# Rearranging the GpSimd work, two weight sums, the product order and the start of a ReGLU MLP kernel

## The chip, the cores and the metric

The kernel runs on one core of one Trainium2 chip. The metric is the device time of one execution in microseconds (us). Every kernel here was also run once under the hardware profiler; the page, timeline and waits quoted below are from that execution, and their times count from its first instruction.

Engines: PE is TensorE's matmuls (PEld its weight loads), DVE is VectorE, ACT is ScalarE, POOL is GpSimd, SP is the engine that issues most transfers. In the profile's lines, SPq is SP's sequencer.

## The reference

```python
batch, seq, dim, hidden = 16, 256, 512, 2048      # x 4096x512, w1 512x4096, w2 2048x512, float32

def reference(x, w1, w2):
    h = x @ w1
    gate, value = np.split(h, 2, axis=-1)
    h = np.maximum(gate, 0) * value
    return (h @ w2).astype(np.float32)
```

## The kernel before

The kernel computes in float16 with Strassen's scheme: seven products P1 to P7 in place of eight, for sums of blocks of the weights (T1 to T4) and of x or g (S1 to S4). The 4096 rows are taken in four rounds of 1024. A round has a first matmul (16 blocks of 7 products, x times w1, giving g) and a second matmul, called mm2 (4 pairs of 7 products, g times w2). While TensorE works, the other engines form the sums, evict the PSUM tiles, check that the values fit float16's range, and fetch the next round's x.

The next round's x comes in two transfers: GpSimd starts a "cast" (float32 in HBM to a float16 copy in HBM, 1024 rows each), and then SP starts eight transposing loads from that copy. The range checks on x (`look`) read the same float16 copies.

```python
    def look(t, at):                       # range check of 256 rows of x, all on GpSimd
        n, m = t.shape[1:]
        fold = tmp.tile([P, n, m], F32, name="fold", tag="fold", bufs=1)
        nc.gpsimd.tensor_tensor(fold, t, t, op=MULT)
        while m > 2:
            m //= 2
            nc.gpsimd.tensor_tensor(fold[:, :, :m], fold[:, :, :m], fold[:, :, m:2 * m], op=ADD)
        nc.gpsimd.tensor_tensor(st[:, at:at + n], fold[:, :, 0], fold[:, :, 1], op=ADD)

    def sums_of(o, eng=nc.vector):         # S sums: VectorE, or GpSimd where eng says so
        for n, i0, i1, op in (("S1", "A21", "A22", ADD), ("S2", "S1", "A11", SUB), ("S4", "A12", "S2", SUB),
                              ("S3", "A11", "A21", SUB)):
            yield eng.tensor_tensor(o[n], o[i0], o[i1], op=op)
    # [...]
    def look_x(s, i):
        look(load_rows(s, i), 32 * s + 8 * i)      # the rows are fetched where the check stands
    # [...]
    for n, at in enumerate([(1, jb) for jb in (0, 2, 4, 6, 13)] + [(2, jb) for jb in (0, 2, 4, 6, 13)] +
                           [(3, jb) for jb in range(6)]):
        LOOKX[at] = n // 4, n % 4
    CASTS = {(0, 12): 1, (1, 0): 0, (1, 1): 2, (1, 8): 3}      # (round, block): which 1024 rows are cast
    SUMS = (9, 10, 11, 12)                                     # blocks of the next round's x sums on GpSimd
    SUMS_AT = (10, 11, 13, 15), (22, 26, 36, 40), (46, 53, 57, 61), (70, 78, 82, 87)   # steps of the S sums in mm2
    # [...] in the loop over the first matmul of round 0:
                    if 6 <= todo < 10:                         # w2's four blocks, loaded by GpSimd
                        n2 = ("B11", "T3", "B22", "B21")[todo - 6]
                        nc.gpsimd.dma_start(out=vop[n2], in_=w2_v[(0, 0, 1, 1)[todo - 6], (0, 1, 1, 0)[todo - 6]])
                    if todo == len(wl):
                        nc.gpsimd.tensor_tensor(vop["T1"], vop["T3"], vop["B11"], op=SUB)
                        nc.gpsimd.tensor_tensor(vop["T2"], vop["B22"], vop["T1"], op=SUB)
                        for j in range(0, NPLAIN, 2):
                            plain_w_end(j, 2)                  # four sums of 128x512 on GpSimd
                        nc.gpsimd.tensor_tensor(vop["T3"], vop["B22"], vop["T3"], op=SUB)
    # [...]
    ORDER = ("P1 0, P1 1, P2 0, P2 1, P1 2, P5 0, P2 2, P6 0, P3 0, P7 0, P5 1, P6 1, P4 0, P3 1, P7 1, P5 2, P4 1, "
             "P6 2, P3 2, P7 2, P1 3, P4 2, P5 3, P2 3, P6 3, P3 3, P7 3, P4 3")   # mm2: product, pair
```

The start of round 0 is special: x is transposed on TensorE (`turn_first`), and the first two blocks use eight ordinary products per half of the rows (`Plain`) because no sums are ready yet.

```python
    turn_first(xo, 0, 0, new_w())
    turn_first(xo, 0, 1, new_x())
    rest()
    ys = [psy.tile([P, TH], F32, name="Y", tag="Y") for _ in range(3)]
    plain[0].products(0, *first_half, half)
    turn_first(xo, 0, 2, new_x())
    turn_first(xo, 0, 3, ys[0])
    plain[0].products(0, *first_half, other)
    # [...] second half likewise; clear(ys[i]) are three filler matmuls
```

## Time and profile before

| | before |
|---|---|
| median of 4 runs | 325.98 us (324.76 to 326.54) |
| profiled span | 323.4 us |
| TensorE busy | 305.7 us, 95% |
| first product of the Strassen kind | 18.88 us |
| first mm2 begins | 63.12 us |
| mm2 stretch of rounds 1, 2, 3 | 28.46, 29.86, 24.45 us |
| first-matmul stretch of rounds 2, 3 | 48.65, 48.64 us |

An "mm2 stretch" runs from the first product of mm2 to the first product of the next round; a "first-matmul stretch" from there to the next mm2. They are read from the starts of TensorE's rows in the timeline. Rounds 1 to 3 do the same TensorE work in mm2, so round 3, which has no idle time, shows the length that the others could have.

The first mm2 in the timeline of the kernel before. Columns: start, duration, engine, line, operation, output and inputs, count; in brackets the idle time before it and what ended it.

```profile
66.53 0.61 PE L314 MATMUL X<-v_B_95,g 128*128 128x256 f16 x4 [1.07 <-DMA v_B_95<-in_w_dram]
...
67.70 4.05 POOL L555 TENSOR_TENSOR v_T_99<-v_B_96,v_T_99 128x2048 f16<-128x2048 f16 x1
...
68.39 3.91 DVE L160 TENSOR_TENSOR w_stage<-g 128x1024 f16<-128x1024 f16 x1
...
72.36 1.05 PE L314 MATMUL W<-v_T_97,w_stage 128*128 128x256 f16 x8 [2.61 <-DVE w_stage L160]
72.39 0.69 DVE L160 TENSOR_TENSOR w_stage<-w_stage,g 128x1024 f16<-128x1024 f16 x1
```

Compare the two VectorE rows: the same operation on the same shapes takes 3.91 us while GpSimd's T3 sum runs, and 0.69 us right after it. The VectorE sum ends within 0.6 us of GpSimd's. TensorE waits 2.61 us for it.

The second mm2 in the timeline of the kernel before:

```profile
147.02 2.57 POOL L160 TENSOR_TENSOR x_S_1145<-x_A_1140,x_S_1145 128x1024 f16<-128x1024 f16 x1
147.64 2.50 DVE L160 TENSOR_TENSOR w_stage<-g,w_stage 128x1024 f16<-128x1024 f16 x1
...
150.19 1.05 PE L314 MATMUL W<-v_B_96,w_stage 128*128 128x256 f16 x8 [1.48 <-ACT sq L175]
151.96 5.87 POOL L169 TENSOR_TENSOR fold<-fold 128x512 f32<-128x512 f32 x6
152.49 1.47 PE L314 MATMUL Y<-v_T_99,w_stage 128*128 128x256 f16 x8 [1.25 <-DVE w_stage L160]
...
154.16 1.89 PE L314 MATMUL W<-v_T_97,w_stage 128*128 128x256 f16 x8 [0.20 <-DVE w_stage L160]
```

GpSimd is still busy with x sums and one late check, VectorE's sums last 2.5 us, TensorE idles, and after the idling a group of eight matmuls lasts 1.89 us instead of 1.05: its clock has dropped. The wait at 150.19 is put down to ScalarE, but these matmuls do not read what that ScalarE row (a range check on w1) wrote; they read `w_stage`, and the VectorE sum that ends at 150.14 is the one to look at.

### The profile page before, as it was taken

To read this page: it belongs to the slowest core of one execution; us is meant where nothing else is said; L and a number is where in the kernel's file an instruction comes from. 1 tells how busy PE (TensorE), PEld (TensorE's weight loads), DVE (VectorE), ACT (ScalarE), POOL (GpSimd) and SP (SyncE) were. 2 spreads that over 40 slices of the span, in tenths; PEclk is the share of its full clock that TensorE was granted. 3 is DMA by queue.
4 is the path that set the end of the run, shared out by engine and by line. 5 is a ranking of instruction groups with operands and counts; after the bars stand their busy time and mean duration, and the time that the engine had idled before them with its cause. 6 is when DMAs were issued, how large, how long until landed. Compare 5 with 4: busy or idle time off the path is not lost.

```text
span 323.4 us, 5208 instructions
## 1 busy us (share of the span) xinstructions
PE 305.7 (95%) x1870; PEld 183.5 (57%) x1870; DVE 239.0 (74%) x372; ACT 175.7 (54%) x350; POOL 166.1 (51%) x191
## 2 busy tenths in 40 slices
PE   7879999959999999996999999999999999999992
PEld 3744444548864444464785444448885444447882
DVE  1478888879748888889935888888735888898741
ACT  2468886516675555534476455554676555553230
POOL 2299999990024008999505179991005898700000
PEclk9999999999999999999899999999999999999998
DMA  8985758978536252060224430000235300000223
GB/s 247 356 252 184 238 90 110 197 105 170 183 117 130 53 134 77 2 130 0 90 107 132 100 127 3 0 1 2 84 113 172 89 2 1 0 2 1 84 80 105
DMA packets 37199, 32.90 MB, mean 102 GB/s; under 512 B 14384, under 2 KB 32048, under 8 KB 37040
## 3 DMA queue, kind: packets, MB, share of 16 engines
q1 hardware_dynamic: 31760, 25.70, 25.8%
q0 software_dynamic: 4352, 6.29, 11.6%
q10 hardware_dynamic: 1056, 0.52, 0.6%
q8 instruction: 16, 0.26, 0.4%
q14 instruction: 15, 0.12, 0.1%
HBM read 27.26 MB, written 12.58 MB: 123 GB/s over the span
## 4 chain that ended last, share of the span: by engine, by line
PE 73%; POOL 9%; DMA 8%; DVE 5%; issue 3%; SPq 0%; ACT 0%; DVEq 0%; POOLq 0%
PE Y L229 20%; PE W L229 13%; PE X L229 13%; PE Y L314 12%; PE W L314 8%; PE X L314 7%; DVE w_stage L160 4%; DMA v_B_95<-in_w_dram 4%; POOL w_T_90 L211 3%; POOL w_T_91 L212 3%; POOL w_T_93 L214 2%; DMA w_stage<-in_w_dram 2%; DMA x_S_122<-in_x_dram 2%; POOL w_T_92 L213 0%; DVE g L266 0%
## 5 line engine op out<-in xcount | busy, mean ns | idle before, releaser
L166 POOL TENSOR_TENSOR fold<-xh 128x1024 f32<-128x1024 f16 x16 | 30.7, 1920 | 93.6 <-DMA xh<-x_1069 43.3
L256 DVE SCALAR_TENSOR_TENSOR cc<-W,pu 128x512 f32<-128x512 f32 x62 | 42.9, 691 | 32.3 <-ACT pu L250 29.8
L314 PEld LDWEIGHTS <-w_stage 128*128 128x128 f16 x512 | 50.4, 99 | 13.7 <-DVE w_stage L160 7.4
L169 POOL TENSOR_TENSOR fold<-fold 128x512 f32<-128x512 f32 (+2 forms) x96 | 54.0, 562 | 7.5
L236 ACT COPY Y<-X 128x512 f32<-128x512 f32 x62 | 35.4, 570 | 38.4 <-PE X L229 22.3
L250 ACT ACTIVATE pu<-Y 128x512 f32<-128x512 f32 x62 | 37.0, 597 | 35.2 <-PE Y L229 34.1
L266 DVE SCALAR_TENSOR_TENSOR g<-Y,cc 128x512 f16<-128x512 f32 x62 | 42.2, 681 | 4.3 <-PE Y L229 4.3
L257 DVE SCALAR_TENSOR_TENSOR g<-X,cc 128x512 f16<-128x512 f32 x62 | 42.9, 691 | 2.3
L314 PEld LDWEIGHTS <-g 128*128 128x128 f16 x384 | 37.5, 98 | 9.5 <-DMA v_B_95<-in_w_dram 1.3
L262 DVE SCALAR_TENSOR_TENSOR cc<-Y,pu 128x512 f32<-128x512 f32 x62 | 42.2, 681 | 0.1
L243 ACT ACTIVATE pu<-W 128x512 f32<-128x512 f32 x62 | 37.4, 603 | 0.4 <-DVE g L257 0.4
L160 DVE TENSOR_TENSOR w_stage<-g 128x1024 f16<-128x1024 f16 x32 | 27.2, 878 | 0.2
L229 PEld LDWEIGHTS <-w_B_89 128*128 128x128 f16 x124 | 12.0, 98 | 15.8 <-DVE x_S_153 L160 1.6
L229 PEld LDWEIGHTS <-w_T_93 128*128 128x128 f16 x124 | 12.0, 97 | 15.3 <-issue 2.5
L229 PEld LDWEIGHTS <-w_T_91 128*128 128x128 f16 x124 | 12.1, 98 | 15.0 <-issue 0.5
L229 PEld LDWEIGHTS <-w_T_90 128*128 128x128 f16 x124 | 12.1, 98 | 14.7
L229 PEld LDWEIGHTS <-w_B_88 128*128 128x128 f16 x124 | 12.1, 98 | 14.5 <-issue 0.6
L229 PEld LDWEIGHTS <-w_T_92 128*128 128x128 f16 x124 | 12.1, 98 | 14.2 <-POOL w_T_91 L212 0.6
L314 PE MATMUL W<-v_T_97,w_stage 128*128 128x256 f16 x128 | 17.5, 282 | 2.8 <-DVE w_stage L160 2.8
L229 PEld LDWEIGHTS <-w_B_87 128*128 128x128 f16 x124 | 12.0, 96 | 13.3
L314 PE MATMUL Y<-v_T_99,w_stage 128*128 128x256 f16 x128 | 17.0, 277 | 1.3 <-DVE w_stage L160 1.3
L314 PE MATMUL W<-v_B_96,w_stage 128*128 128x256 f16 x128 | 16.6, 273 | 1.5 <-ACT sq L175 1.5
(220 smaller groups left out, 578.3 us busy)
## 6 DMA issues: line engine op xcount, KB each, us to landing
out_dram<-o SPq DMA_DIRECT2D x31, 256.0 KB, 2.0
w_stage<-in_w_dram SPq DMA_DIRECT2D x14, 512.0 KB, 5.3
x_625<-in_x_dram POOLq DMA_DIRECT2D x1, 1024.0 KB, 10.4
x_1069<-in_x_dram POOLq DMA_DIRECT2D x1, 1024.0 KB, 7.9
xh<-x_1069 SPq DMA_DIRECT2D x4, 256.0 KB, 3.4
x_1112<-in_x_dram POOLq DMA_DIRECT2D x1, 1024.0 KB, 7.4
xh<-x_625 SPq DMA_DIRECT2D x4, 256.0 KB, 3.0
x_1344<-in_x_dram POOLq DMA_DIRECT2D x1, 1024.0 KB, 7.5
```

Source lines behind the costliest of these rows:

```text
L160: yield eng.tensor_tensor(o[n], o[i0], o[i1], op=op)
L166: nc.gpsimd.tensor_tensor(fold, t, t, op=MULT)
L169: nc.gpsimd.tensor_tensor(fold[:, :, :m], fold[:, :, :m], fold[:, :, m:2 * m], op=ADD)
L229: nc.tensor.matmul(ps, wop[wn][:, b, self.jb * P:(self.jb + 1) * P], self.xo[xn][:, b, :], start=fresh and b == 0, stop=b == 1, skip_group ...
L236: nc.scalar.copy(out=self.Y, in_=self.X)
L243: nc.scalar.activation(self.p5, self.W, COPY, scale=GS)
L250: nc.scalar.activation(self.u2, self.Y, COPY, scale=GS)
L256: nc.vector.scalar_tensor_tensor(out=self.c12, in0=self.W, scalar=GS, in1=self.u2, op0=MULT, op1=ADD)
L257: nc.vector.scalar_tensor_tensor(out=self.g[:, self.jb, :TH], in0=self.X, scalar=0.0, in1=self.c12, op0=MAX, op1=MULT)
L262: nc.vector.scalar_tensor_tensor(out=self.c22, in0=self.Y, scalar=GS, in1=self.p5, op0=MULT, op1=ADD)
L266: nc.vector.scalar_tensor_tensor(out=self.g[:, self.jb, TH:], in0=self.Y, scalar=0.0, in1=self.c22, op0=MAX, op1=MULT)
L314: nc.tensor.matmul(ps, self.op[an][:, i], vop[wn][:, i], start=name in ("P1", "P5") and i == 0, stop=i == NJ // 2 - 1, skip_group_check=True)
```

## The change

Its intent is to leave GpSimd idle during mm2. Checks follow one another early in the first matmul, with their rows fetched ahead; casts 0 and 2 come right behind cast 1; T3 and the plain blocks' sums go to VectorE, and the first mm2 gets an order of products that uses T3 and T4 late. At the start, four blocks of x are turned before the first product.

```diff
-    halfs = ctx.enter_context(tc.tile_pool(name="halfs", bufs=4))
-    tmp = ctx.enter_context(tc.tile_pool(name="tmp", bufs=4))
+    halfs = ctx.enter_context(tc.tile_pool(name="halfs", bufs=3))
+    tmp = ctx.enter_context(tc.tile_pool(name="tmp", bufs=6))
 [...] Plain.products: its last VectorE instruction becomes a method of its own, gate(h)
-    ORDER = ("P1 0, P1 1, P2 0, P2 1, P1 2, P5 0, P2 2, P6 0, P3 0, P7 0, P5 1, P6 1, P4 0, P3 1, P7 1, P5 2, P4 1, "
+    ORDER = ("P1 0, P1 1, P2 0, P2 1, P1 2, P5 0, P2 2, P6 0, P3 0, P7 0, P5 1, P6 1, P3 1, P7 1, P4 0, P5 2, P4 1, "
              "P6 2, P3 2, P7 2, P1 3, P4 2, P5 3, P2 3, P6 3, P3 3, P7 3, P4 3")
+    FIRST_ORDER = ("P1 0, P1 1, P2 0, P2 1, P1 2, P5 0, P2 2, P6 0, P3 0, P5 1, P6 1, P3 1, P5 2, P6 2, P3 2, P7 0, P7 1, "
+                   "P4 0, P7 2, P4 1, P1 3, P4 2, P5 3, P2 3, P6 3, P3 3, P7 3, P4 3")
 [...] start (second half of the rows likewise; the three filler matmuls go)
     turn_first(xo, 0, 0, new_w())
     turn_first(xo, 0, 1, new_x())
     rest()
+    turn_first(xo, 0, 2, new_x())
+    turn_first(xo, 0, 3, new_w())
     plain[0].products(0, *first_half, half)
-    turn_first(xo, 0, 2, new_x())
-    turn_first(xo, 0, 3, ys[0])
 [...] checks
-        look(load_rows(s, i), 32 * s + 8 * i)
+        look(rows.pop(0), 32 * s + 8 * i)
-    [(1, jb) for jb in (0, 2, 4, 6, 13)] + [(2, jb) for jb in (0, 2, 4, 6, 13)] + ...
+    [(1, jb) for jb in (0, 2, 4, 6, 8)] + [(2, jb) for jb in (0, 2, 4, 6, 8)] + ...
+                if n == "P1" and s and jb in (0, 3 if s == NS - 1 else 6):
+                    wanted = [LOOKX[s, j] for j in range(NJ) if (s, j) in LOOKX]
+                    rows += [load_rows(*r) for r in (wanted[3:] if jb else wanted[:3])]
-    CASTS = {(0, 12): 1, (1, 0): 0, (1, 1): 2, (1, 8): 3}
-    SUMS = (9, 10, 11, 12)
+    CASTS = {(0, 11): 1, (0, 13): 0, (0, 14): 2, (1, 8): 3}
+    SUMS = (10, 11, 12, 13)
 [...] w2's blocks are loaded one weight group earlier; then, on GpSimd, only
+                if (s, n, jb) == (0, "P7", 13):
+                    nc.gpsimd.tensor_tensor(vop["T1"], vop["T3"], vop["B11"], op=SUB)
+                    nc.gpsimd.tensor_tensor(vop["T2"], vop["B22"], vop["T1"], op=SUB)
 [...] and on VectorE, at steps of the first mm2
+            for n2, i0, i1, at in (("T3", "B22", "T3", (46, 50)), ("T4", "B21", "T2", (57, 58))):
+                for i, u in enumerate(at):
+                    part = [vop[n][:, i * NJ // 4:(i + 1) * NJ // 4] for n in (n2, i0, i1)]
+                    job(u, lambda part=part: nc.vector.tensor_tensor(*part, op=SUB))
+            for i, u in enumerate((74, 78, 82, 83)):
+                job(u, lambda i=i: plain_w_end(0, NPLAIN, i))
 [...] steps of the S sums: a SUMS_FIRST for the first mm2, one line of SUMS_AT earlier
```

More of the change, by code (lines that the diff above doesn't have):

```diff
@@ L286, in products, with gate @@
             if cols[1] == TH:
-                v = tmp.tile([P, 2, TH], F32, name="v", tag="tmp")[:, 0]
+                self.v = v = tmp.tile([P, 2, TH], F32, name="v", tag="tmp")[:, 0]
                 nc.scalar.activation(v, self.W, COPY, scale=GS)
-                nc.vector.scalar_tensor_tensor(out=self.g[:, self.jb, h * TH:(h + 1) * TH], in0=self.X, scalar=0.0,
-                                               in1=v, op0=MAX, op1=MULT)
+        def gate(self, h):
+            nc.vector.scalar_tensor_tensor(out=self.g[:, self.jb, h * TH:(h + 1) * TH], in0=self.X, scalar=0.0,
+                                           in1=self.v, op0=MAX, op1=MULT)
     s_place = w_stage[:, :4].rearrange("p u v -> p (u v)").bitcast(F16).rearrange("p (i n h t) -> p i n h t", i=2, n=4, t=P)
@@ L354, in P4 @@
             self.send(1, slice(0, DO // 2 if self.end else DO))
-    ORDER = ("P1 0, P1 1, P2 0, P2 1, P1 2, P5 0, P2 2, P6 0, P3 0, P7 0, P5 1, P6 1, P4 0, P3 1, P7 1, P5 2, P4 1, "
+    ORDER = ("P1 0, P1 1, P2 0, P2 1, P1 2, P5 0, P2 2, P6 0, P3 0, P7 0, P5 1, P6 1, P3 1, P7 1, P4 0, P5 2, P4 1, "
              "P6 2, P3 2, P7 2, P1 3, P4 2, P5 3, P2 3, P6 3, P3 3, P7 3, P4 3")
+    FIRST_ORDER = ("P1 0, P1 1, P2 0, P2 1, P1 2, P5 0, P2 2, P6 0, P3 0, P5 1, P6 1, P3 1, P5 2, P6 2, P3 2, P7 0, P7 1, "
+                   "P4 0, P7 2, P4 1, P1 3, P4 2, P5 3, P2 3, P6 3, P3 3, P7 3, P4 3")
     LAST_ORDER = ORDER.replace("P1 3, P4 2, P5 3, P2 3, P6 3, P3 3, P7 3", "P1 3, P5 3, P2 3, P6 3, P4 2, P7 3, P3 3")
     def mm2_stream(s, pairs):
-        for step in (LAST_ORDER if s == NS - 1 else ORDER).split(", "):
+        for step in (LAST_ORDER if s == NS - 1 else ORDER if s else FIRST_ORDER).split(", "):
             name, t = step.split()
@@ L402, in plain_w, with plain_w_end @@
         return lambda: nc.scalar.copy(out=wop["B22"][:, :, js], in_=t[:, 1, :, 1])
-    def plain_w_end(jb, n):
+    def plain_w_end(jb, n, i):
+        n2, i0, i1 = (("T1", "T3", "B11"), ("T2", "B22", "T1"), ("T3", "B22", "T3"), ("T4", "B21", "T2"))[i]
         js = slice(jb * P, (jb + n) * P)
-        op = {n: w[:, :, js] for n, w in wop.items()}
-        nc.gpsimd.tensor_tensor(op["T1"], op["T3"], op["B11"], op=SUB)
-        nc.gpsimd.tensor_tensor(op["T2"], op["B22"], op["T1"], op=SUB)
-        nc.gpsimd.tensor_tensor(op["T3"], op["B22"], op["T3"], op=SUB)
-        nc.gpsimd.tensor_tensor(op["T4"], op["B21"], op["T2"], op=SUB)
+        nc.vector.tensor_tensor(wop[n2][:, :, js], wop[i0][:, :, js], wop[i1][:, :, js], op=SUB)
     g = g_set[0]
@@ L444, in fast_way @@
     first_half, second_half = (xo["A11"], xo["A12"]), (xo["A21"], xo["A22"])
+    half, other = (0, TH // 2), (TH // 2, TH)
     rest = plain_w(0)
@@ L448, in fast_way @@
     rest()
-    half, other = (0, TH // 2), (TH // 2, TH)
-    ys = [psy.tile([P, TH], F32, name="Y", tag="Y") for _ in range(3)]
+    turn_first(xo, 0, 2, new_x())
+    turn_first(xo, 0, 3, new_w())
     plain[0].products(0, *first_half, half)
-    turn_first(xo, 0, 2, new_x())
-    turn_first(xo, 0, 3, ys[0])
-    plain[0].products(0, *first_half, other)
     plain_w(1)()
     fetch(4, nc.sync)
-    plain[1].products(0, *first_half, half)
-    turn_first(xo, 1, 0, ys[1])
-    turn_first(xo, 1, 1, ys[2])
-    plain[1].products(0, *first_half, other)
-    clear(ys[0])
-    turn_first(xo, 1, 2, new_x())
-    turn_first(xo, 1, 3, new_w())
+    plain[0].products(0, *first_half, other)
+    plain[0].gate(0)
+    plain[1].products(0, *first_half)
+    ps = [new_x(), new_w()]
+    for b in range(4):
+        turn_first(xo, 1, b, ps[b % 2])
+        if b == 1:
+            plain[1].gate(0)
     sums = sums_of(xo)
@@ L467, in fast_way @@
     fetch(5, nc.sync)
+    next(sums)
     plain[0].products(1, *second_half, half)
-    plain[1].products(1, *second_half, half)
     next(sums)
-    clear(ys[1])
-    clear(ys[2])
+    next(sums)
     plain[0].products(1, *second_half, other)
-    next(sums)
+    plain[0].gate(1)
     prepare(3)
-    plain[1].products(1, *second_half, other)
-    next(sums)
+    plain[1].products(1, *second_half)
+    plain[1].gate(1)
     next(sums)
@@ L512, in count @@
         nc.vector.tensor_scalar(out=flag, in0=ps[:1, :1], scalar1=n - 0.5, scalar2=None, op0=LT)
-    for n, at in enumerate([(1, jb) for jb in (0, 2, 4, 6, 13)] + [(2, jb) for jb in (0, 2, 4, 6, 13)] +
-                           [(3, jb) for jb in range(6)]):
+    ats = [(1, jb) for jb in (0, 2, 4, 6, 8)] + [(2, jb) for jb in (0, 2, 4, 6, 8)] + [(3, jb) for jb in range(6)]
+    for n, at in enumerate(ats):
         LOOKX[at] = n // 4, n % 4
+    rows = []
     LOOKS = {}
@@ L523, in fast_way @@
     TAIL = 4
-    CASTS = {(0, 12): 1, (1, 0): 0, (1, 1): 2, (1, 8): 3}
-    SUMS = (9, 10, 11, 12)
-    SUMS_AT = (10, 11, 13, 15), (22, 26, 36, 40), (46, 53, 57, 61), (70, 78, 82, 87)
+    CASTS = {(0, 11): 1, (0, 13): 0, (0, 14): 2, (1, 8): 3}
+    SUMS = (10, 11, 12, 13)
+    SUMS_FIRST = (10, 11, 13, 45), (17, 22, 26, 53), (33, 37, 41, 64), (67, 72, 76, 80)
+    SUMS_AT = (10, 11, 13, 15), (22, 26, 30, 36), (46, 53, 57, 61), (70, 78, 82, 87)
     for s in range(NS):
@@ L546, in fast_way @@
                         prepare(todo)
-                    if 6 <= todo < 10:
-                        n2 = ("B11", "T3", "B22", "B21")[todo - 6]
-                        nc.gpsimd.dma_start(out=vop[n2], in_=w2_v[(0, 0, 1, 1)[todo - 6], (0, 1, 1, 0)[todo - 6]])
-                    if todo == len(wl):
-                        nc.gpsimd.tensor_tensor(vop["T1"], vop["T3"], vop["B11"], op=SUB)
-                        nc.gpsimd.tensor_tensor(vop["T2"], vop["B22"], vop["T1"], op=SUB)
-                        for j in range(0, NPLAIN, 2):
-                            plain_w_end(j, 2)
-                        nc.gpsimd.tensor_tensor(vop["T3"], vop["B22"], vop["T3"], op=SUB)
+                    if 5 <= todo < 9:
+                        n2 = ("B11", "T3", "B22", "B21")[todo - 5]
+                        nc.gpsimd.dma_start(out=vop[n2], in_=w2_v[(0, 0, 1, 1)[todo - 5], (0, 1, 1, 0)[todo - 5]])
+                if (s, n, jb) == (0, "P7", 13):
+                    nc.gpsimd.tensor_tensor(vop["T1"], vop["T3"], vop["B11"], op=SUB)
+                    nc.gpsimd.tensor_tensor(vop["T2"], vop["B22"], vop["T1"], op=SUB)
                 if n == "P1" and jb == (14 if s == 0 else 2) and s + 1 < NS:
@@ L581, in job @@
             jobs.setdefault(at, []).extend(what)
-        for t, at in enumerate(SUMS_AT):
+        for t, at in enumerate(SUMS_AT if s else SUMS_FIRST):
             sums = sums_of(pairs[t].op)
@@ L587, in fast_way @@
         if s == 0:
-            for i, u in enumerate((19, 32)):
-                half = [vop[n][:, i * NJ // 4:(i + 1) * NJ // 4] for n in ("T4", "B21", "T2")]
-                job(u, lambda half=half: nc.vector.tensor_tensor(*half, op=SUB))
+            for n2, i0, i1, at in (("T3", "B22", "T3", (46, 50)), ("T4", "B21", "T2", (57, 58))):
[4 more added lines that the diff above has]
+                job(u, lambda i=i: plain_w_end(0, NPLAIN, i))
         if s + 1 < NS:
```

## The prediction

> **What bounds it now.** TensorE: the page gives it 95% busy, 305.7 of 323.4 us, and 73% of the chain of waits. The timeline shows that the four first-matmul stages run without gaps once started (48.65 us each in the second and third), so only the gaps can be won.
>
> - Second matmul (mm2), first to next stage's first product: 28.46, 29.86 and 24.45 us in the first three rounds. The third has no TensorE gap, so it is the floor: 4.0 us too much in the first, 5.4 in the second.
> - The start: first Strassen product at 18.88 us, then 1.8 us of gaps up to 26 us.
> - The tail after the last matmul, about 6 us, is not touched.
>
> **Why.** In the first mm2 a VectorE sum of 128x1024 takes 3.91 us instead of 0.68 while GpSimd runs its 4.05 us T3 sum; TensorE waits 2.6 us for it. Before that it waits 1.1 us for the w2 block B21, which landed 12.5 us after issue, behind an x cast. In the second mm2 GpSimd runs x sums and one late check until 158.5 us; five VectorE sums take 1.6 to 2.5 us, TensorE idles 3.2 us, and its clock falls (0.83 in that stretch: one eight-matmul group took 1.89 instead of 1.04 us). The check is late because its rows landed only at 121.9 us, queued behind the x transposes. The Trainium skill, SBUF — State Buffer, "Who interferes with whom", says that a VectorE instruction with two SBUF inputs fully blocks against a GpSimd instruction reading SBUF; these durations agree.
>
> **What the change does.**
> 1. Second mm2: five checks of 5.95 us start at once (rows fetched first), then four x sums of 2.1 us: GpSimd ends about 7 us before mm2. Worth 5.2 us, on the critical path.
> 2. First mm2: T3, T4 and the plain-block sums move to VectorE (about 4 us added at 0.68 and 0.35 us each; it has room), their users come later, B21 is issued before the casts and should land near 58 us. GpSimd ends T2 near 64 us. Worth up to 4.0 us.
> 3. Start: all four blocks turned first, three filler matmuls gone, three sums ahead of the gates: first Strassen product near 17.8 us, fewer gaps. Worth 2 us.
> 4. Cost: casts 0 and 2 now follow cast 1 directly. In the profile two transposes issued at 71.2 and 72.5 us landed only when cast 0 had (79.6), and the next issue was held 6.5 us. The transposes for the second round may so be held until about 74 to 78 us and land at 82 to 87, just where mm2, now ending near 85.5, needs their sums; the output sends queue behind them. I take 1 us back.
>
> Sum: 5.2 + 4.0 + 2.0 − 1.0 = 10.2 us.
>
> **Predicted: 316.0 us, 8 in 10 between 313.3 and 320.5.** Faster by over 2%: 0.90; within 2%: 0.09; slower: 0.01.
>
> **Right if:** the second mm2 takes 24.5 us with GpSimd idle and VectorE's 128x1024 sums at 0.68 us throughout; the first mm2 takes 24.5 to 26 us; no wait for B21; the second round's first product starts at 85 to 88 us (before: 91.58); the third and fourth rounds unchanged at 73.1 us apart.
>
> **Wrong if:** VectorE waits several us for the second round's transposed x (second round's start at 89 to 91, mm2 cold): the first mm2's gain is given back and the time is near 320. Or four queued casts and loads hold GpSimd itself, so that T1 and T2 come late and overlap VectorE's sums. Or VectorE, with more sums in the first mm2, becomes its limit. Or GpSimd's weight sums, whose first input lands at 15.1 us, hold the earlier start back (gain 1 instead of 2 us).

## The result and the profile after

| | before | after |
|---|---|---|
| median | 325.98 us (4 runs) | 315.75 us (4 runs, 315.18 to 316.62) |
| profiled span | 323.4 us | 313.5 us |
| TensorE busy | 305.7 us, 95% | 303.6 us, 97% |
| first Strassen product | 18.88 us | 19.21 us |
| first mm2 begins | 63.12 us | 62.31 us |
| mm2 stretch, rounds 1, 2, 3 | 28.46, 29.86, 24.45 us | 24.44, 24.65, 24.64 us |
| second round begins | 91.58 us | 86.75 us |

The ratio is 0.9694, with a 95% interval of 0.9655 to 0.9732. Ratios are the mean time of one kernel's fast runs over that of the other's of the same rounds, so they are not quite the ratio of the medians quoted. In a later job the changed kernel was timed again: ratio 0.9675 (0.9646 to 0.9705). All outputs are right.

The span shrank by 9.9 us: 0.8 at the start, 4.0 in the first mm2, 5.2 in the second, and 0.2 lost in the third. The line of shares by engine in the chain of waits says the same; the first line is before, and after it follows in its own fence.

```profile
PE 73%; POOL 9%; DMA 8%; DVE 5%; issue 3%; SPq 0%; ACT 0%; DVEq 0%; POOLq 0%
```

```profile
PE 91%; DVE 4%; DMA 2%; ACT 1%; SPq 0%; issue 0%; DVEq 0%
```

GpSimd's 9% and most of the DMA share left the chain: GpSimd's weight sums, the wait for the w2 block B21 and the sums behind it no longer lead to the last instruction.

The first mm2 after, in the timeline (L316 is the line of mm2's matmuls here, L592 of the two w2 sums on VectorE):

```profile
60.41 4.08 POOL L553 TENSOR_TENSOR v_T_98<-v_B_96,v_T_97 128x2048 f16<-128x2048 f16 x1
...
66.33 0.69 DVE L160 TENSOR_TENSOR w_stage<-g 128x1024 f16<-128x1024 f16 x1
...
73.57 0.68 DVE L592 TENSOR_TENSOR v_T_99<-v_B_96,v_T_99 128x1024 f16<-128x1024 f16 x1
...
82.70 0.69 DVE L160 TENSOR_TENSOR x_S_664<-x_S_666,x_A_663 128x1024 f16<-128x1024 f16 x1
...
86.75 0.59 PE L229 MATMUL X<-x_A_661,w_B_87 128*128 128x512 f16 x2
```

GpSimd ends T2 at 64.49 us, before VectorE's first S sum; that sum now takes 0.69 us, and T3 costs VectorE two instructions of 0.68 us. No TensorE row of this stretch shows a wait.

The second mm2 after: GpSimd's last x sum, and VectorE's second S sum in mm2.

```profile
126.65 2.13 POOL L160 TENSOR_TENSOR x_S_1129<-x_A_1124,x_S_1129 128x1024 f16<-128x1024 f16 x1
...
140.10 0.69 DVE L160 TENSOR_TENSOR w_stage<-w_stage,g 128x1024 f16<-128x1024 f16 x1
```

GpSimd is done 6.6 us before mm2 begins at 135.39.

The change has a price in the transfers. SP's rows of the timeline, first before, then after:

```profile
63.91 2.52 SPq L189 DMA_TRANSPOSE x_A_687<-x_625  x2
66.52 2.52 SPq L189 DMA_TRANSPOSE x_A_688<-x_625  x2
69.14 3.35 SPq L189 DMA_TRANSPOSE x_S_692<-x_625  x2
72.54 7.80 SPq L189 DMA_TRANSPOSE x_A_689<-x_625  x2
```

```profile
65.08 2.53 SPq L189 DMA_TRANSPOSE x_A_661<-x_578  x2
67.70 8.25 SPq L189 DMA_TRANSPOSE x_A_662<-x_578  x2
76.04 2.52 SPq L189 DMA_TRANSPOSE x_S_666<-x_578  x2
78.61 2.56 SPq L189 DMA_TRANSPOSE x_A_663<-x_578  x2
81.27 5.66 SPq L324 DMA_DIRECT2D out_dram<-o  x7
```

Two transposes normally take 2.5 us to issue. Before, the last pair took 7.80 us, across cast 0. Now the second pair takes 8.25 us, and the first pair, issued from 65.1 us, needed 10.2 and 11.0 us to land. The casts, in the list of DMA issues of the profile after (columns: size, us from issue to landing):

```profile
x_578<-in_x_dram POOLq DMA_DIRECT2D x1, 1024.0 KB, 10.3
x_633<-in_x_dram POOLq DMA_DIRECT2D x1, 1024.0 KB, 14.8
x_676<-in_x_dram POOLq DMA_DIRECT2D x1, 1024.0 KB, 19.9
```

With issues at 54.70, 55.23 and 55.73, they landed at 65.0, 70.0 and 75.6 us. The first pair of transposes landed 0.5 and 1.0 us after the last cast. The rest were still in time: the last was issued at 79.9 and landed 2.7 us later, and VectorE took up its first x sum at 82.70 without a recorded wait. There is hardly any margin there.

What held them can be read from the DMA queues between 66 and 73 us (columns: packets, MB, share of the 16 engines; q0 carries the casts, q1 the transposes):

```profile
q0 software_dynamic: 62, 1.51, 103.0%
q1 hardware_dynamic: 28, 0.01, 0.7%
```

The data itself stood, and not only the report of its landing. In the packet records of the trace a packet of a cast is 32 KB and takes about 2.5 us; one of a transpose is 256 bytes and takes 0.02 to 0.03 us. In these 7 us the casts moved 1.5 MB and the transposes 7 KB.

### The profile page after: what moved, and what is told of

It reads as the page before. It is cut to its first block, busy times and chain, and to the rows that moved or that the text cites. A ratio compares the mean times of both kernels' runs of the same rounds, so it can differ in the third digit from the quotient of the medians.

```text
span 313.5 us, 5175 instructions
## 1 busy us (share of the span) xinstructions
PE 303.6 (97%) x1851; PEld 181.9 (58%) x1851; DVE 231.9 (74%) x378; ACT 176.0 (56%) x350; POOL 154.3 (49%) x186
## 4 chain that ended last, share of the span: by engine, by line
PE 91%; DVE 4%; DMA 2%; ACT 1%; SPq 0%; issue 0%; DVEq 0%
PE Y L229 25%; PE X L229 16%; PE W L229 16%; PE Y L316 13%; PE W L316 9%; PE X L316 9%; DMA x_S_122<-in_x_dram 2%; PE X L284 1%; PE W L284 1%; DVE x_S_151 L160 1%; DVE x_S_153 L160 0%; DVE x_S_150 L160 0%; DVE cc L256 0%; DVE g L257 0%; DVE x_S_152 L427 0%; SPq L421 0%
## 5 line engine op out<-in xcount | busy, mean ns | idle before, releaser
L169 POOL TENSOR_TENSOR fold<-fold 128x512 f32<-128x512 f32 (+2 forms) x96 | 51.8, 540 | 7.5
L316 PEld LDWEIGHTS <-w_stage 128*128 128x128 f16 x512 | 50.1, 98 | 6.2 <-issue 0.4
L316 PEld LDWEIGHTS <-g 128*128 128x128 f16 x384 | 37.5, 98 | 8.2
L160 DVE TENSOR_TENSOR w_stage<-g 128x1024 f16<-128x1024 f16 x32 | 21.3, 685 | 0.2
L229 PEld LDWEIGHTS <-w_T_91 128*128 128x128 f16 x124 | 12.1, 98 | 14.6
L316 PE MATMUL Y<-v_T_100,g 128*128 128x256 f16 x128 | 17.1, 273 | 0.0
L316 PE MATMUL Y<-v_T_98,w_stage 128*128 128x256 f16 x128 | 16.6, 273 | 0.0
L316 PE MATMUL W<-v_B_96,w_stage 128*128 128x256 f16 x128 | 16.6, 273 | 0.0
```

The lines of the kernel that those rows point to most:

```text
L229: nc.tensor.matmul(ps, wop[wn][:, b, self.jb * P:(self.jb + 1) * P], self.xo[xn][:, b, :], start=fresh and b == 0, stop=b == 1, skip_group ...
L316: nc.tensor.matmul(ps, self.op[an][:, i], vop[wn][:, i], start=name in ("P1", "P5") and i == 0, stop=i == NJ // 2 - 1, skip_group_check=True)
```

## The experiments

Twelve runs followed, eleven of other kernels and one of the changed kernel again. Stretches in this table are from each kernel's own profiled execution. Kernels with one run were only looked at: their state (fast or slow) is not known, so their verdicts rest on single stretches of the trace, not on the time. All other runs compared are fast ones.

| run | median us (runs) | ratio to before, 95% | first mm2 begins | mm2 stretches 1, 2, 3 |
|---|---|---|---|---|
| before | 325.98 (4) | | 63.12 | 28.46, 29.86, 24.45 |
| after | 315.75 (4) | 0.9694 (0.9655 to 0.9732) | 62.31 | 24.44, 24.65, 24.64 |
| e1_checks | 320.83 (4) | 0.9862 (0.982 to 0.9903) | 64.52 | 27.22, 24.45, 24.44 |
| e2b_oldchecks | 321.14 (4) | 0.9866 (0.9823 to 0.991) | 62.14 | 24.44, 29.72, 24.63 |
| e2_late | 315.76 (1) | | 61.99 | 24.44, 24.63, 24.65 |
| e3_t3 | 319.23 (1) | | 60.91 | 28.99, 24.64, 24.63 |
| e7_read | 319.87 (1) | | 62.93 | 24.44, 24.64, 27.51 |
| e8_write | 316.2 (1) | | 62.22 | 24.44, 24.64, 24.64 |
| e6_cast3 | 322.09 (1) | | 60.81 | 24.44, 24.63, 24.63 |
| e4_oldstart | 316.7 (4) | 0.9729 (0.9688 to 0.9769) | 62.16 | 24.45, 24.64, 24.63 |
| e5_warm | 315.47 (5) | 0.968 (0.9663 to 0.9696) | 60.83 | 24.45, 24.64, 24.63 |
| after_again | 315.0 (6) | 0.9675 (0.9646 to 0.9705) | 60.91 | 24.44, 24.64, 24.65 |
| e9_both | 314.91 (6) | 0.9668 (0.9634 to 0.9702) | 60.85 | 24.45, 24.45, 24.45 |
| e10_gate | 321.06 (6) | 0.9863 (0.9829 to 0.9897) | 62.0 | 24.44, 24.45, 24.44 |

The theory at this point: the gain is GpSimd's absence from mm2, because a GpSimd sum and a VectorE sum block each other. Rivals: the gain comes from the deeper buffers, the new order of products, the earlier loads, or the new start.

### e1_checks: the checks alone, on the kernel before

```diff
-        look(load_rows(s, i), 32 * s + 8 * i)
+        look(rows.pop(0), 32 * s + 8 * i)           # rows fetched at blocks 0 and 6, as in the change
-    [(1, jb) for jb in (0, 2, 4, 6, 13)] + [(2, jb) for jb in (0, 2, 4, 6, 13)] + ...
+    [(1, jb) for jb in (0, 2, 4, 6, 8)] + [(2, jb) for jb in (0, 2, 4, 6, 8)] + ...
-    CASTS = {(0, 12): 1, (1, 0): 0, ...}
+    CASTS = {(0, 12): 1, (0, 15): 0, ...}           # only so that cast 0 is written ahead of its rows
-    SUMS = (9, 10, 11, 12)
+    SUMS = (10, 11, 12, 13)
```

> The kernel before with one part of the change alone: the check rows of a round are fetched in two batches ahead of their use, and the five checks follow one another (blocks 0, 2, 4, 6, 8), with the four GpSimd x sums behind them. First matmul, first mm2 and start stay as before. If GpSimd work inside the second mm2 is what stretched it: the second mm2 falls from 29.9 to 24.5 us, its VectorE sums all take 0.68 us, and the kernel is 5 us faster (ratio near 0.984), the first mm2 unchanged at 28.5 us. Rival, that the second mm2 is slow for its own reasons (clock, sends, buffers): it stays above 28 us.

Measured: the second mm2 took 24.45 us, all of VectorE's sums there 0.69 us or less, and the time fell by 5.0 us in the medians (325.83 of the same job to 320.83; the interval of the ratio lies below 1). Buffers, order and start are those of the kernel before, so the place of the checks, with the x sums behind them, is worth about half of the change. GpSimd was not quite out of this mm2: its last x sums ran until 143.1 us, 2.7 us into it, and cost nothing, because VectorE's first sum there began at 144.36.

The first mm2 was expected at 28.5 us and took 27.22. It began 1.4 us later than in the kernel before, so the block B21, which landed at 66.58 us, was in time, and only the wait for the sum beside T3 (2.61 us) was left.

### e2_late: an experiment that did not do what it said

```diff
-    [(1, jb) for jb in (0, 2, 4, 6, 8)] + ...
+    [(1, jb) for jb in (0, 2, 4, 14, 15)] + ...
-                if n == "P1" and s and jb in (0, 3 if s == NS - 1 else 6):
+                if n == "P1" and s and jb in (0, 3 if s == NS - 1 else 14 if s == 1 else 6):
```

> The changed kernel, only that in the second round the last two checks and the fetch of their rows come at blocks 14 and 15, so that GpSimd runs them from about 132 to 145 us, into the second mm2 (135.4 on). GpSimd's x sums are done before. If GpSimd's reads during mm2 are the cause: the VectorE sums between 139 and 145 us take 1.5 to 2.5 us, TensorE waits 1 to 3 us, second mm2 26 to 28 us instead of 24.65. Rival, that the x sums on GpSimd (not the checks) did the harm in the kernel before: second mm2 stays below 25 us.

Measured: second mm2 24.63 us, but GpSimd had ended its last check at 128.6 us, before mm2. Neither SP nor GpSimd waits for TensorE's place in the program: the fetches written at block 14 went out at 101.2 and 101.9 us, in the fifth of the round's sixteen blocks. The run says nothing about the cause. It does show that on these engines a place in the program is no time unless data ties it to one.

### e2b_oldchecks: the checks of the kernel before in the changed kernel

```diff
-        look(rows.pop(0), 32 * s + 8 * i)
+        look(load_rows(s, i), 32 * s + 8 * i)
-    CASTS = {(0, 11): 1, (0, 13): 0, (0, 14): 2, (1, 8): 3}
-    SUMS = (10, 11, 12, 13)
+    CASTS = {(0, 11): 1, (1, 0): 0, (1, 1): 2, (1, 8): 3}
+    SUMS = (9, 10, 11, 12)
 # and the blocks (0, 2, 4, 6, 13) and the fetch at the check, as before
```

> The changed kernel with the rows, checks, x sums and casts of the kernel before; the first mm2 and the start stay as changed. This replaces the run in which the late fetch was not late. If GpSimd in the second mm2 is the cause: GpSimd ends inside it again, VectorE's sums there take 1.6 to 2.5 us, second mm2 28 to 30 us instead of 24.64, kernel 4 to 5.5 us slower than the changed one (320 to 321 us). Rival, that the gain came from the deeper buffers or the new order of products: second mm2 below 26 us.

Measured: second mm2 29.72 us, 321.14 us in all, 6.1 us above the changed kernel of the same job (4 to 5.5 were expected; mm2 itself is longer by 5.1). The timeline of that mm2:

```profile
140.37 2.49 DVE L160 TENSOR_TENSOR w_stage<-w_stage,g 128x1024 f16<-128x1024 f16 x1
142.89 2.49 DVE L160 TENSOR_TENSOR w_stage<-g,w_stage 128x1024 f16<-128x1024 f16 x1
144.80 2.34 POOL L166 TENSOR_TENSOR fold<-xh 128x1024 f32<-128x1024 f16 x1
...
147.21 5.48 POOL L169 TENSOR_TENSOR fold<-fold 128x512 f32<-128x512 f32 x6
```

The old picture is back, with six buffers and the new order in place. The rivals fall for the second mm2.

### e3_t3: T3 back on GpSimd in the first mm2

```diff
                     nc.gpsimd.tensor_tensor(vop["T2"], vop["B22"], vop["T1"], op=SUB)
+                    nc.gpsimd.tensor_tensor(vop["T3"], vop["B22"], vop["T3"], op=SUB)
-            for n2, i0, i1, at in (("T3", "B22", "T3", (46, 50)), ("T4", "B21", "T2", (57, 58))):
+            for n2, i0, i1, at in (("T4", "B21", "T2", (57, 58)),):
```

> The changed kernel with the w2 sum T3 back on GpSimd, right behind T2; its users stay late. If the exclusive use of a shared path by a GpSimd and a VectorE sum stretched the first mm2: GpSimd runs T3 from about 64.5 to 68.6 us, the VectorE sum that should start at 66.3 lasts until about 69 (2.5 us instead of 0.69), TensorE waits 1 to 2 us for it, first mm2 25.5 to 26.5 us. Rival, that T3 came late for its first user in the kernel before: no wait here, because T3 is ready ten us ahead of P7, first mm2 24.4 us.

Measured, in the timeline of that mm2:

```profile
64.36 4.04 POOL L554 TENSOR_TENSOR v_T<-v_B,v_T 128x2048 f16<-128x2048 f16 x1
...
64.94 4.01 DVE L160 TENSOR_TENSOR w_stage<-g 128x1024 f16<-128x1024 f16 x1
...
69.01 1.05 PE L316 MATMUL W<-v_T,w_stage 128*128 128x256 f16 x8 [2.70 <-DVE w_stage L160]
69.89 1.54 PE L316 MATMUL X<-v_B,g 128*128 128x256 f16 x8
71.22 1.91 PE L316 MATMUL Y<-v_T,w_stage 128*128 128x256 f16 x8
```

One GpSimd sum, whose result was wanted only eleven us later, brought the whole loss of the first mm2 back: 28.99 us. The size was expected too small. VectorE's sum began 0.6 us into GpSimd's, so it lost the full 3.3 us; and of the 4.55 us that mm2 grew, 2.7 are the wait and 1.7 are the four groups from 69.01 to 74.18, which took 5.17 us where four take 3.49. The mean granted clock from 70 to 75 us was 0.66. So a stall can cost more than its length, but it need not: the kernel before and e1 waited 2.61 us for the same sum, their recorded clock stayed at 1.00, and e1's mm2 was longer by 2.78 us in all.

### e7_read and e8_write: what in GpSimd's work blocks VectorE

```diff
+        if s == 2:                                  # third mm2, where GpSimd has nothing to do
+            def busy():
+                d = tmp.tile([P, 2, 512], F32, name="d", tag="fold", bufs=1)
+                d = d[:, 0], d[:, 1]
+                nc.scalar.copy(out=d[0][:, :1], in_=st[:, :1])       # ties the work to this place
+                nc.gpsimd.memset(d[0], 1.0)
+                for i in range(8):
+                    nc.gpsimd.tensor_tensor(d[1], d[0], d[0], op=ADD)        # e7_read
+                    # e8_write: nc.gpsimd.memset(d[1], float(i)); nc.gpsimd.memset(d[0], float(i))
+            job(10, busy)
```

> The changed kernel with dummy GpSimd work in the third mm2 (otherwise free of it): after a small ScalarE copy at its step 10, one memset and eight tensor_tensor additions of 128x512 float32, which read SBUF (8 to 10 us in all); results unused. If GpSimd sums that read SBUF stop VectorE sums with two SBUF inputs: VectorE's 128x1024 sums between 212 and 222 us take 1.2 us or more instead of 0.68, TensorE waits, third mm2 25.5 to 28 us instead of 24.64. Rival, that only large or fp16 GpSimd sums do it: no change.

> As the run with eight additions, with sixteen GpSimd memsets of 128x512 float32 in their place, which write SBUF and read nothing. If it is GpSimd's reading that stops VectorE: the sums stay at 0.68 us and third mm2 at 24.6 us. Rival, that any GpSimd instruction with SBUF traffic does it: the sums stretch as with the additions.

Measured for the additions:

```profile
212.76 11.16 POOL L602 TENSOR_TENSOR d<-d 128x512 f32<-128x512 f32 x8
...
214.38 1.41 DVE L160 TENSOR_TENSOR w_stage<-w_stage,g 128x1024 f16<-128x1024 f16 x1
...
221.64 1.05 PE L316 MATMUL Y<-v_T,w_stage 128*128 128x256 f16 x8 [0.40 <-DVE w_stage L160]
```

Measured for the memsets:

```profile
212.84 0.52 POOL L602 MEMSET d<- 128x512 f32 x1
213.25 0.69 DVE L160 TENSOR_TENSOR w_stage<-w_stage,g 128x1024 f16<-128x1024 f16 x1
```

Eight additions, even small float32 ones, doubled VectorE's sums to 1.41 us and stretched the third mm2 to 27.51 us. Sixteen memsets in the same place left the sums at 0.69 and mm2 at 24.64 us, although they ran without a break until 219.4 us, beside nine of the sums. It is GpSimd's reading that matters here. This agrees with the Trainium skill, SBUF — State Buffer, "Who interferes with whom", by which a VectorE instruction with two SBUF inputs contends with a GpSimd instruction that reads SBUF and not with one that only writes it.

### e6_cast3: the margin of the transposes

```diff
-    CASTS = {(0, 11): 1, (0, 13): 0, (0, 14): 2, (1, 8): 3}
+    CASTS = {(0, 11): 1, (0, 13): 0, (0, 14): 2, (0, 15): 3}
```

> The changed kernel with the fourth cast of x issued in the first round too (behind T2, at about 64.5 us), as a fourth in the queue. In the changed kernel the transposes of round 2 stood until cast 2 landed at 75.6 us, and VectorE took their sums up at 82.7 without a wait. If transposes stand while casts are under way: they stand until about 81, the last lands near 88, VectorE waits about 5 us for x, the second round starts 4 to 7 us later than 86.75, total 320 to 323 us. Rival, that the queues share by turns: transposes land before 84 us and the start stays within 1 us.

Measured: 322.09 us, in the expected range. The first four transposes took 15.94 us to issue, and none landed before the fourth cast had (80.2 us). VectorE's row:

```profile
88.31 1.42 DVE L160 TENSOR_TENSOR x_S<-x_S,x_A 128x1024 f16<-128x1024 f16 x2 [7.03 <-DMA x_A<-x]
```

The first product of the round, which needs no sum, was not late (85.25 us); the loss fell behind it, in a first-matmul stretch of 56.78 us where others take 48.65. So transposes all but stand still under casts, the back-to-back casts were a real risk, and the change as made stays just on the safe side of it. The rival's premise was not false: the packet records show the queues in turns, 76 packets of transposes beside 80 of the cast's 32 KB from 64.8 to 77.5 us. But at 256 bytes a packet that is 19 KB against 2.5 MB.

### e4_oldstart, e5_warm and after_again: the start

```diff
 # e4_oldstart: the start of the kernel before, in the changed kernel
 # e5_warm:
     turn_first(xo, 0, 0, new_w())
+    for i in range(3):
+        clear(ys[i])                               # filler matmuls, 512 columns each
     turn_first(xo, 0, 1, new_x())
+    for i in range(4):
+        clear(ys[i % 3])
     rest()
     turn_first(xo, 0, 2, new_x())
```

> The changed kernel with the start of the kernel before (turns of x between half products, three filler matmuls, gates right behind their products). The prediction put the new start at 2 us: then this kernel takes 317.7 us. The two traces put it at 0.8 us (first mm2 begins at 62.31 instead of 63.12): then 316.5 us, first mm2 beginning at 63.1, and the clock at 1.00 in the first 10 us instead of 0.88. Both mm2 stretches stay at 24.4 to 24.7 us.

> The changed kernel with seven filler matmuls (512 columns) in the two waits for x at the start: three behind the first turn, four behind the second. The trace of the changed kernel shows TensorE idle 0.7 and 0.9 us there, and then the products from 8.6 to 11 us at 0.43 us a pair instead of 0.22. If that idling is what lowered the clock: clock 1.00 in the first 10 us, first product stretch 1 to 1.5 us shorter, first mm2 at about 61.2 instead of 62.3 us, kernel 0.5 to 1.2 us faster than the changed one. Rival, that the x sums on VectorE, slowed by GpSimd's weight sums, bind the start: the products run warm but the first mm2 still begins at 62.0 or later.

> The changed kernel itself again, beside the runs that follow, for a comparison on one chip and for a second look at its start. The traces so far have the first mm2 begin between 60.8 and 62.9 us in kernels whose start is that of the changed one, so this one begins in that range too; time 315 to 316.5 us; second and third mm2 24.64 us again.

The two traces alone had suggested a gain of 0.8 us at the start. That reading was too fine. Eight traces of kernels with the new start and no filler (after, e2, e2b, e3, e6, e7, e8, after_again) have the first mm2 begin between 60.81 and 62.93 us, on average at 61.78. Three with the old start (before, e1, e4) lie between 62.16 and 64.52, on average at 63.27. The averages differ by 1.5 us, with ranges that overlap, and before and e1 differ from the changed kernel in more than the start; the times of e4 (0.9729) and of the changed kernel (0.9694) have overlapping intervals too. e4 did not follow the second reading either: its first mm2 began at 62.16 us, where 63.1 was expected. What varies is TensorE's speed in the first products. TensorE rows of the timeline, first after, then after_again, the same kernel:

```profile
7.72 1.11 PE L425 MATMUL W<-ident,x_S_122 128*128 128x128 f32 x4
8.63 0.63 PE L284 MATMUL X<-x_A_147,w_B_87 128*128 128x256 f16 x2
9.05 0.63 PE L284 MATMUL W<-x_A_147,w_T_92 128*128 128x256 f16 x2
```

```profile
7.72 0.66 PE L425 MATMUL W<-ident,x_S 128*128 128x128 f32 x4
8.21 0.38 PE L284 MATMUL X<-x_A,w_B 128*128 128x256 f16 x2
8.43 0.38 PE L284 MATMUL W<-x_A,w_T 128*128 128x256 f16 x2
```

Pairs start 0.42 us apart in the one and 0.22 in the other. Sorted by this spacing the traces agree: of the eight, e3, e6 and after_again start at 0.22 and reach the first mm2 at 60.81 to 60.91 us, the other five start at 0.42 and reach it at 61.99 to 62.93. e4 starts at 0.22 and reaches it at 62.16. At equal speed, then, the new start gained about 1.3 us, on one trace of the old start; the two traces compared at first were a fast start before and a slow one after. Speed is not all that varies: e10, below, also starts at 0.22 and reaches its first mm2 only at 62.0, after waits at 20 to 23 us for an x sum and a weight copy.

The Trainium skill, TensorE: Matmul & The Clock Gate, "What's actually happening", says that the default state of the clock is throttled and activity releases it, and that the window it watches is free-running, so that one kernel can start differently from run to run. These two traces agree.

The fillers of e5 gave the early case (60.83 us), as in three of eight traces without them; e9 and e10, which have them too, also start at 0.22, so the fillers' part is likely and not shown. They did not make the kernel measurably faster (0.5 to 1.2 us were expected), since its interval contains the changed kernel's ratio. Part of the reason is in the next stretch: with an early start the first matmul of the second round took 49.25 us in e5 and 49.36 in after_again instead of 48.64, because x's transposes land when the casts allow it, whatever TensorE has gained. The transfers took 0.6 to 0.7 us back (0.8 in e9, below).

### e9_both and e10_gate: looking for a better version

```diff
 # e9_both: the fillers of e5_warm, and in rounds 2 to 4 the ORDER of the kernel before
 # e10_gate: e9_both, and
-    CASTS = {(0, 11): 1, (0, 13): 0, (0, 14): 2, (1, 8): 3}
+    CASTS = {(0, 11): 1, (1, 8): 3}
+                if n == "P1" and (s, jb) == (0, 15):
+                    seen = tmp.tile([P, 1], F16, name="seen", tag="seen", bufs=1)
+                    nc.gpsimd.tensor_copy(out=seen, in_=xo_next["A22"][:, 1, :1])   # waits for the transposes
+                    cast_x(0)
+                    cast_x(2)
```

> The changed kernel with the seven filler matmuls at the start and, in rounds 2 to 4, the order of products of the kernel before (P4 of pair 0 ahead of P3 and P7 of pair 1). The changed kernel's second and third mm2 take 24.64 us where the kernel before takes 24.45 in its third. If the new order costs these 0.19 us: second and third mm2 24.45 us, and the second round's start stays at about 85.3 with a wait for x sums of about 0.6 us behind it; kernel 0.4 us faster than the run with fillers alone. Rival, that the later P4 is not the cause: 24.64 us stays.

> As the run before it, and casts 0 and 2 of x are held on GpSimd, by a one-column copy from the last transposed x tile, until the transposes of round 2 have landed. In the changed kernel the transposes stood until cast 2 landed at 75.6 us. If only the casts held them: the last transpose is issued by 75 us and landed by 78, VectorE takes the x sums at its turn, the first matmul of the second round takes 48.65 us instead of 49.25, check rows land by 87 us; kernel 0.4 to 0.7 us faster than the run before it, about 314.6 us. Rival: row checks or the transposes of round 3 come late and the second mm2 stretches again.

e9: second and third mm2 fell to 24.45 us each, so the later P4 does cost 0.19 us a round; but with 314.91 us against 315.0 for the changed kernel in the same job, the timed runs can't tell the two apart.

e10 failed: 321.06 us. Its transposes were indeed free (all issued by 75.9 us), but the casts now ran from 77 us on, across the output writes of the first mm2. Landing of an output write took up to 14.6 us, where the longest in the changed kernel was 4.0. Outputs and first-matmul temporaries share buffers, and so two engines stood:

```profile
93.92 0.69 DVE L256 SCALAR_TENSOR_TENSOR cc<-W,pu 128x512 f32<-128x512 f32 x1 [6.85 <-DMA out_dram<-o]
...
94.53 0.60 ACT L243 ACTIVATE pu<-W 128x512 f32<-128x512 f32 x1 [3.86 <-DMA out_dram<-o]
```

The first-matmul stretch grew to 53.77 us. The early casts of the change use a time in which nothing else is urgent; moving them to help one transfer hurts another. No run here is shown to beat the changed kernel.

## Why the prediction was right

The predicted 316.0 us stands against 315.75 measured, and the mechanism was the one stated. Term by term:

| term | predicted | measured |
|---|---|---|
| second mm2 | 5.2 us | 5.2 in the two traces; 5.0 by time in e1 alone; e2b gives it back |
| first mm2 | 4.0 us | 4.0 in the two traces; 2.8 between e1, which has no wait for B21, and after; e3 returns 4.55 with T3 alone |
| start | 2 us | 0.8 in the two traces; about 1.3 between traces whose first products run at the same speed, on one trace of the old start |
| transposes behind casts | −1.0 us | 0 in the profiled run, −0.6 to −0.8 where the start was early |
| new order in rounds 2 and 3 | not named | −0.2 us in each |

- **GpSimd's reads against VectorE's sums, first and second mm2: right, and shown from both sides.** Adding GpSimd reads to an mm2 stretches it (e2b, e3, e7), adding GpSimd writes does not (e8), and removing the reads mends it (e1). Of the first mm2's 4.0 us, about 2.8 belong to this (e1 against after) and the rest to B21.
- **B21: right, with a slip.** TensorE no longer waits for it (1.07 us before). It landed at 60.1 us instead of near 58, because GpSimd issued it at 53.8; the first product that needs it came later still.
- **VectorE has room: right.** In the first mm2 from 70 to 80 us it is busy 9.92 of 10 us, yet TensorE did not wait for it. The sums added there came to 3.0 us (two of 0.68 and four of 0.42) and not to 4, because T4 had been VectorE's before.
- **Start: over-sized.** The gain was put at 2 us; it is about 1.3 at equal speed of the first products, and not resolved in the timed runs. The first Strassen product came at 19.21 us in the profiled run, where "near 17.8" was predicted; in after_again it came at 17.61. What I left out is that turning four blocks first makes TensorE wait for x (0.7 and 0.9 us), and that its first products then ran at the low rate in five of eight traces.
- **Transposes: the mechanism right, the size at its edge.** They were held until 75.6 us and landed at 82.6, inside the predicted 74 to 78 and 82 to 87; the packets show why (above). That this cost nothing in the profiled run is luck of about a tenth of a us: e6 shows 7 us of waiting from one more cast.
- **"Third and fourth rounds unchanged at 73.1 us apart": slightly wrong.** They are 73.29 apart. e9 shows that the moved P4 is the cause.

So the total is closer than its parts deserve: the start fell short by 0.7 to 1.2 us and the transposes took back less than I allowed.

## What to carry to other kernels

Read the length of a stage in a round where nothing disturbs it, and compare its other rounds with that: the difference is what a rearrangement can win, and here it gave 9.2 of the 9.9 us in advance. Keep GpSimd instructions that read SBUF out of any stretch where VectorE adds two SBUF tiles on the critical path, even if their results are not urgent. GpSimd writes were free here, and so was a place early in the first matmul: VectorE's instructions there read one input from PSUM, and none between 86 and 140 us of the changed kernel took more than 0.69 us with the checks beside them. When transfers are bunched to make room, look for what shares the engines with them at that time, and remember that a place in the program moves a transfer only if some data holds it there.

## What the Trainium skill lacked or had wrong

- DMA: Bandwidth & Descriptors, "Queues, rings and completion order", says that each engine takes turns between the queues it has work for, packet by packet. The packet records agree, but what such turns cost when the packets are unlike is not stated there: beside packets of 32 KB from GpSimd's casts, a transposing load moved 7 KB in 7 us (after, 66 to 73 us). Two loads issued from 65.1 us needed 11.0 and 10.2 us to land, where later ones in the same trace need 2.6 to 2.7; a fourth cast held the issue of four transposes for 15.94 us (e6), and plain output writes beside casts took up to 14.6 us (e10). The same section also says that the write that reports a transfer lands only after all earlier writes of that engine, across its queues; that alone does not explain the delay, since the packets of the data were held too.
- SBUF — State Buffer, "Who interferes with whom", calls the loser fully blocked; the runs agree for one long sum (3.91 us instead of 0.69). It does not spell out what a train of short ones does: with eight GpSimd additions the two engines went on in turns, 1.41 us a sum (e7).
- TensorE: Matmul & The Clock Gate, "What's actually happening", puts the low clock after an idle window of about 3.4 us. Here less was enough: a wait of 2.70 us in e3, where mm2 grew by 4.55 us in all, and waits of 1.48 and 1.25 us close together in before (second mm2). But a single wait of 2.61 us left the recorded clock at 1.00 and the matmuls at their pace in before and e1 (first mm2). The page also warns ("Seeing it yourself") that recorded clock events can be unreliable, and a run agrees: e1's record reads 1.00 from 5 to 12.5 us although pairs started 0.42 us apart from 7.4 us on, which is the low rate; the spacing of matmuls is the safer reading.
